# Closing the Tile frame behind the first transfer, and x in another shape and order, in a batched-expert kernel

## The chip, the core and the metric

The kernel runs on one core of a Trainium2 chip. Its time is the device time of one execution in microseconds (us). The span of a profile, from the first instruction to the last, is a little shorter than the time of the same execution. An engine here is one of TensorE (PE, its weight loads PEld), VectorE (DVE), ScalarE (ACT), GpSimd (POOL) and SyncE (SP). "q" behind a name (SPq, POOLq) marks the engine's instruction queue: semaphores, branches, drains, DMA issues.

## What is computed

```python
# x: 8 experts x 256 tokens x 512, w1: 8 x 512 x 2048, w2: 8 x 2048 x 512, all float32
h = np.matmul(x, w1)
h = np.maximum(h, 0)
return np.matmul(h, w2)          # 8 x 256 x 512, float32
```

## The kernel before

**Data.** The weights are float32 in HBM and arrive as bfloat16: POOL issues their DMAs, which convert on the way. `load_w1(e)` (L95) fetches 2 MB (counted as bfloat16) into one of two buffers, `load_w2(e)` (L98) the same; for the last expert w2 is fetched in two pieces (L103, L104). Each of 128 partitions gets one contiguous row of 16 KB per transfer, read from 32 KB in HBM. All of POOL's DMAs run through one queue (q0), in order; SP's run through another (q1). Both queues feed the same 16 DMA engines.

**x.** Experts 0 to 3 are fetched by SP as float32 (`x_f`, L82), experts 4 to 7 by POOL as bfloat16 (`x_c`, L106), each as one contiguous row of eight tokens per partition, 16 KB of HBM. ACT and DVE each bring one half into `x_b` (L156, L173; for the second group L160, L177). PE transposes `x_b` in four steps of eight 128x128 blocks (L203); DVE and ACT copy the four results out of PSUM in turns (`take_x`, L135; L147 and L145) into `xt`. Since eight tokens in a row lie in one partition, the tokens of one expert come out of the transposition scattered, and the copies write with a step of four elements (`"p m (q l) -> p l m q"`, L143). Both groups go through this before expert 0 begins; `give_xe` (L149) then copies one expert's columns into one of two buffers `xe`, which PE reads.

**Experts.** For each expert PE does 64 matmuls of the first layer (L215), in four quarters that go through two PSUM tensors; ACT and DVE apply the relu (L167, L185). Then come 32 matmuls of the second layer (L232), whose results DVE and ACT copy into `out_sb` (L189, L169).

**Order of the loads.** POOL issues x_c, w1(0), w2(0), builds the identity (L109 to L119), issues w1(1), w2(1), and then for each further expert waits until PE is done with the buffer: w1(e) is issued when the first layer of expert e-2 is done (L123), w2(e) when its second layer is done (L125). After the last weight it issues the outputs of experts 0 to 5 (L129) and of 6 (L132). SP stands in a row of waits (L83 to L89): each time a weight has landed it wakes and gives PE a token (`t_w`). Behind these waits it waits for the last result (L90, L91), issues the last expert's output (L92) and waits for all three outputs (L242).

**The frame.** The program stands inside a Tile frame (L269) and, in it, inside a critical section (L59) in which nothing is scheduled automatically. On entry SP signals the other engines (L59). On leaving, all engines report to SP (L59), then come, under L269, a drain of every engine, a barrier of all five, a clearing of the frame's semaphores by POOL, and a second barrier. The barrier at L258 is the program's own, ahead of the frame.

Of the kernel before, what the change touches and what calls it, by code (L numbers as in the profile page):

```python
# [9 lines left out]
def kernel(  # L10
# [48 lines left out]
    with tc.tile_critical(no_gpsimd_drain=True):  # L59
        sem = nc.alloc_semaphore  # L60
        s_x = [sem(f"s_x{g}") for g in range(2)]
        s_w1 = [sem(f"s_w1_{e}") for e in range(E)]
        s_w2 = [sem(f"s_w2_{e}") for e in range(E)]
        s_w2b = sem("s_w2b")
        s_out = [sem(f"s_out{i}") for i in range(3)]
        s_id = sem("s_id")
        s_act = sem("s_act")
        s_dve = sem("s_dve")
        s_tr = sem("s_tr")
        s_h = sem("s_h")  # L70
        s_o = sem("s_o")
        t_xb = sem("t_xb")
        t_pt = [sem(f"t_pt{b}") for b in range(2)]
        t_xe = sem("t_xe")
        t_w = sem("t_w")
        t_ha = sem("t_ha")
        t_hb = sem("t_hb")

        sp, pool, act, dve, pe = nc.sync, nc.gpsimd, nc.scalar, nc.vector, nc.tensor


        sp.dma_start(x_f[:], x_rows(0)).then_inc(s_x[0], 16)  # L82
        for e in range(E):  # L83
            sp.wait_ge(s_w1[e], 16).then_inc(t_w, 1)
            if e < E - 1:
                sp.wait_ge(s_w2[e], 16).then_inc(t_w, 2)
            else:
                sp.wait_ge(s_w2[e], 16).then_inc(t_w, 1)
                sp.wait_ge(s_w2b, 16).then_inc(t_w, 1)  # L89
        sp.wait_ge(s_act, E)  # L90
        sp.wait_ge(s_dve, E)  # L91
        sp.dma_start(out_r[:, E - 1], o_sb[:, E - 1]).then_inc(s_out[2], 16)  # L92


        def load_w1(e):  # L95
            pool.dma_start(w1_sb[e % 2][:], w1_r[e]).then_inc(s_w1[e], 16)  # L96

        def load_w2(e):  # L98
            if e < E - 1:
                pool.dma_start(w2_sb[e % 2][:], w2_r[e]).then_inc(s_w2[e], 16)  # L100
            else:
                b = w2_sb[e % 2]
                pool.dma_start(b[:, :CUT], w2_r[e, :, :CUT]).then_inc(s_w2[e], 16)  # L103
                pool.dma_start(b[:, CUT:], w2_r[e, :, CUT:]).then_inc(s_w2b, 16)  # L104

        pool.dma_start(x_c[:], x_rows(1)).then_inc(s_x[1], 16)  # L106
        load_w1(0)
        load_w2(0)
        pool.memset(identity[:], 0.0).then_inc(s_id, 1)  # L109
        pool.wait_ge(s_id, 1)  # L110
        pool.affine_select(
            out=identity[:],
            in_=identity[:],
            compare_op=mybir.AluOpType.not_equal,
            fill=1.0,
            base=0,
            pattern=[[-1, P]],
            channel_multiplier=1,
        ).then_inc(s_id, 1)  # L119
        load_w1(1)  # L120
        load_w2(1)
        for e in range(2, E):
            pool.wait_ge(s_h, NQ * (e - 1))  # L123
            load_w1(e)
            pool.wait_ge(s_o, MT * (e - 1))  # L125
            load_w2(e)
        pool.wait_ge(s_act, E - 2)
        pool.wait_ge(s_dve, E - 2)
        pool.dma_start(out_r[:, :E - 2], o_sb[:, :E - 2]).then_inc(s_out[0], 16)  # L129
# [5 lines left out]
        def take_x(g, half):  # L135

            for k in range(KT1):
                if k % 2 != half:
                    continue
                eng = act if half else dve  # L140
                eng.wait_ge(s_tr, g * KT1 + k + 1)
                src = pt[k % 2][:].rearrange("p (l m) q -> p l m q", m=MT)
                dst = xt[g][:, k].rearrange("p m (q l) -> p l m q", l=G)  # L143
                if half:
                    act.copy(dst, src).then_inc(t_pt[1], 1)  # L145
                else:
                    dve.tensor_copy(dst, src).then_inc(t_pt[0], 1)  # L147

        def give_xe(e):  # L149
            g, i0 = e // G, (e % G) * P  # L150
            dve.tensor_copy(xe[e % 2][:], xt[g][:, :, :, i0:i0 + P]).then_inc(t_xe, 1)  # L151


        HALF = J // 2
        act.wait_ge(s_x[0], 16)
        act.copy(x_b[:, :HALF], x_f[:, :HALF]).then_inc(t_xb, 1)  # L156
        take_x(0, 1)
        act.wait_ge(s_x[1], 16)
        act.wait_ge(s_tr, KT1)
        act.copy(x_b[:, :HALF], x_c[:, :HALF]).then_inc(t_xb, 1)  # L160
        take_x(1, 1)
        s_xt = sem("s_xt")
        act.drain().then_inc(s_xt, 1)  # L163
        for e in range(E):
            for q in range(0, NQ, 2):
                act.wait_ge(s_h, NQ * e + q + 1)
                act.activation(ht[e % 2][:, FB * q:FB * (q + 1), :], ph[0][:], relu).then_inc(t_ha, 1)  # L167
            act.wait_ge(s_o, MT * e + 2)
            act.copy(o_sb[:, e, 1, :], po[1][:]).then_inc(s_act, 1)  # L169


        dve.wait_ge(s_x[0], 16)
        dve.tensor_copy(x_b[:, HALF:], x_f[:, HALF:]).then_inc(t_xb, 1)  # L173
        take_x(0, 0)
        dve.wait_ge(s_x[1], 16)
        dve.wait_ge(s_tr, KT1)
        dve.tensor_copy(x_b[:, HALF:], x_c[:, HALF:]).then_inc(t_xb, 1)  # L177
        take_x(1, 0)
        dve.wait_ge(s_xt, 1)
        give_xe(0)  # L180
        give_xe(1)
        for e in range(E):
            for q in range(1, NQ, 2):
                dve.wait_ge(s_h, NQ * e + q + 1)
                dve.tensor_relu(ht[e % 2][:, FB * q:FB * (q + 1), :], ph[1][:]).then_inc(t_hb, 1)  # L185
            if e + 2 < E:
                give_xe(e + 2)
            dve.wait_ge(s_o, MT * e + 1)
            dve.tensor_copy(o_sb[:, e, 0, :], po[0][:]).then_inc(s_dve, 1)  # L189


        def take(s, n=1):
            pe.wait_ge(s, n).then_inc(s, -n)  # L193

        pe.wait_ge(s_id, 2)
        for b in range(2):
            pe.sem_inc(t_pt[b], 1)
        with pe.Fori(0, 2) as _g:
            take(t_xb, 2)
            for k in range(KT1):  # L200
                take(t_pt[k % 2])
                for j in range(J):
                    ins = pe.transpose(pt[k % 2][:, j], x_b[:, j, k::KT1], identity[:])  # L203
                ins.then_inc(s_tr, 1)

        with pe.Fori(0, E // 2) as _i:
            for b in range(2):
                take(t_xe)
                take(t_w)
                for q in range(NQ):  # L210
                    if q >= 2:
                        pe.wait_ge((t_ha, t_hb)[q % 2], 1)
                    for i in range(FB):
                        for kt in range(KT1):
                            ins = pe.matmul(  # L215
                                ph[q % 2][:, i, :],
                                w1_sb[b][:, kt, FB * q + i::KT2],
                                xe[b][:, kt],
                                start=(kt == 0),
                                stop=(kt == KT1 - 1),  # L220
                            )
                    ins.then_inc(s_h, 1)
                take(t_w)
                for kt in range(KT2):
                    if kt == 2 * FB:
                        take(t_ha, 2)
                    if kt == 3 * FB:
                        take(t_hb, 2)
                    if kt == CUT:
                        take(t_w)  # L230
                    for m in range(MT):
                        ins = pe.matmul(  # L232
                            po[m][:],
                            ht[b][:, kt, m * P:(m + 1) * P],
                            w2_sb[b][:, kt, :],
                            start=(kt == 0),
                            stop=(kt == KT2 - 1),
                        )
                        if kt == KT2 - 1:
                            ins.then_inc(s_o, 1)  # L240

        for s in s_out:  # L242
            sp.wait_ge(s, 16)


# [28 lines left out]
```

## Time and profile before

| | us |
|---|---|
| median of three runs | 184.15 |
| lowest and highest | 183.95, 184.28 |
| the profiled execution, its time | 184.07 |
| the profiled execution, its span | 182.3 |
| PE busy in it | 127.5 |
| DVE, ACT, POOL busy in it | 39.4, 35.7, 11.8 |

In the page of the profile the line that begins with DMA has one digit for each fortieth of the span: the mean busy share of the 16 DMA engines in tenths. GB/s counts the bytes as they are written, so that a float32 weight that lands as bfloat16 counts half of what was read. A "packet" is one row of a transfer on one DMA engine. In rows of a single line of the kernel, the three figures with strokes are the least, median and greatest duration in ns, and behind them stand the first and last start in us.

### The profile page before, as it was taken

Reading aid. Unit: us, or ns where it says so; the run is one execution under the profiler, and the core shown is the slowest. Engines: PE = TensorE matmul, PEld = TensorE weight load, DVE = VectorE, ACT = ScalarE, POOL = GpSimd, SP = SyncE. Lnnn points to the kernel's source line nnn. Section 1 sums busy time; section 2 is a strip of 40 time slices with the busy share of each in tenths; the row PEclk is TensorE's granted clock in tenths of the full one; section 3 lists DMA queues with packets and bytes.
Section 4 is the critical chain, followed back from the end, with each engine's and each line's share of the span. In section 5 each row is a group of like instructions: output and inputs, shape, how many; then the busy total and the mean of one; then the engine's idle time right before and its main releaser. Section 6 shows DMA issues by size and latency. Waiting matters only on the chain. (4 is left out here: it accounts for less than half of the span.)

```text
span 182.3 us, 1915 instructions
## 1 busy us (share of the span) xinstructions
PE 127.5 (70%) x832; PEld 90.0 (49%) x832; DVE 39.4 (22%) x38; ACT 35.7 (20%) x31; POOL 11.8 (6%) x26
## 2 busy tenths in 40 slices
PE   0006143999999794998677695949794989589910
PEld 0005142794794394339633682439642874198400
DVE  0025656023123123010501032012301040104010
ACT  2045856130230122002201220012201220122010
POOL 6100000001101101000101001010104000100000
PEclk9999999999999999699999999978999699999996
DMA  5999999999999999999999999999999999999990
GB/s 162 345 241 230 219 205 209 230 223 212 209 219 226 212 205 219 226 223 201 212 230 223 201 209 230 223 212 205 223 226 212 205 219 226 199 210 230 424 418 25
DMA packets 3810, 40.93 MB, mean 225 GB/s; under 512 B 352, under 2 KB 352, under 8 KB 1504
## 3 DMA queue, kind: packets, MB, share of 16 engines
q0 software_dynamic: 3520, 38.27, 94.2%
q1 hardware_dynamic: 288, 2.62, 4.0%
q8 instruction: 2, 0.03, 0.1%
HBM read 71.30 MB, written 4.19 MB: 414 GB/s over the span
## 5 line engine op out<-in xcount | busy, mean ns | idle before, releaser
L215 PE MATMUL pt_h<-xe,w_sb 128*128 128x256 bf16 x512 | 62.4, 286 | 15.8 <-PEq L193 15.8
L215 PEld LDWEIGHTS pt_h<-xe,w_sb 128*128 128x128 bf16 x512 | 58.6, 146 | 21.3 <-issue 18.9
L232 PE MATMUL pt_o<-w_sb,ht_sb 128*128 128x512 bf16 x256 | 58.2, 387 | 9.4 <-PEq L193 9.4
L232 PEld LDWEIGHTS pt_o<-w_sb,ht_sb 128*128 128x128 bf16 x256 | 25.2, 99 | 40.0 <-issue 12.6
L185 DVE TENSOR_SCALAR ht_sb<-pt_h 128x1024 bf16<-128x1024 f32 x16 | 19.6, 1224 | 61.7 <-PE pt_h L215 61.7
L167 ACT ACTIVATE ht_sb<-pt_h 128x1024 bf16<-128x1024 f32 x16 | 16.4, 1023 | 49.4 <-PE pt_h L215 49.4
L203 PE MATMUL pt_tr<-identity,x_b 128*128 128x128 bf16 x64 | 7.5, 308 | 21.4 <-PEq L193 21.4
L169 ACT COPY out_sb<-pt_o 128x512 f32<-128x512 f32 x8 | 4.7, 586 | 72.9 <-PE pt_o L232 72.9
L203 PEld LDWEIGHTS pt_tr<-identity,x_b 128*128 128x128 bf16 x64 | 6.4, 142 | 22.3 <-issue 22.1
L189 DVE COPY out_sb<-pt_o 128x512 f32<-128x512 f32 x8 | 5.5, 692 | 53.6 <-PE pt_o L232 53.6
L147 DVE COPY xt<-pt_tr 128x1024 bf16<-128x1024 bf16 x4 | 9.7, 2431 | 7.8 <-PE pt_tr L203 7.8
L145 ACT COPY xt<-pt_tr 128x1024 bf16<-128x1024 bf16 x4 | 9.7, 2434 | 6.8 <-PE pt_tr L203 6.8
L96 POOL DMA_DIRECT2D w_sb<-in_w_dram x8 | 4.3, 535 | 78.4 <-PE pt_h L215 78.2
L100 POOL DMA_DIRECT2D w_sb<-in_w_dram x7 | 3.7, 536 | 41.6 <-PE pt_o L232 41.6
L156 ACT CAST x_b<-x_f 128x2048 bf16<-128x2048 f32 x1 | 1.9, 1898 | 9.1 <-DMA x_f<-in_x_dram 9.1
L173 DVE CAST x_b<-x_f 128x2048 bf16<-128x2048 f32 x1 | 1.2, 1227 | 11.3 <-DMA x_f<-in_x_dram 11.3
L151 DVE COPY xe<-xt 128x1024 bf16<-128x1024 bf16 x8 | 3.3, 418 | 0.9 <-ACTq L163 0.9
L160 ACT COPY x_b<-x_c 128x2048 bf16<-128x2048 bf16 x1 | 2.0, 1957 | 0.0
L132 POOL DMA_DIRECT2D out_dram<-out_sb x1 | 0.5, 543 | 18.3 <-ACT out_sb L169 18.3
L156 ACT ACT_TABLE_LOAD x1 | 1.3, 1283 | 0.9 <-SPq L59 0.9
L103 POOL DMA_DIRECT2D w_sb<-in_w_dram x1 | 0.5, 528 | 7.5 <-PE pt_o L232 7.5
L129 POOL DMA_DIRECT2D out_dram<-out_sb x1 | 0.8, 846 | 0.0
(9 smaller groups left out, 2.8 us busy)
## 6 DMA issues: line engine op xcount, KB each, us to landing
w_sb<-in_w_dram POOLq DMA_DIRECT2D x15, 2048.0 KB, 30.3
out_dram<-out_sb POOLq DMA_DIRECT2D x1, 3072.0 KB, 37.7
x_f<-in_x_dram SPq DMA_DIRECT2D x1, 2048.0 KB, 10.3
w_sb<-in_w_dram POOLq DMA_DIRECT2D x1, 1152.0 KB, 27.0
x_c<-in_x_dram POOLq DMA_DIRECT2D x1, 1024.0 KB, 12.2
w_sb<-in_w_dram POOLq DMA_DIRECT2D x1, 896.0 KB, 30.8
out_dram<-out_sb POOLq DMA_DIRECT2D x1, 512.0 KB, 19.9
out_dram<-out_sb SPq DMA_DIRECT2D x1, 512.0 KB, 4.8
```

Source lines behind the costliest of these rows:

```text
L96: pool.dma_start(w1_sb[e % 2][:], w1_r[e]).then_inc(s_w1[e], 16)
L100: pool.dma_start(w2_sb[e % 2][:], w2_r[e]).then_inc(s_w2[e], 16)
L145: act.copy(dst, src).then_inc(t_pt[1], 1)
L147: dve.tensor_copy(dst, src).then_inc(t_pt[0], 1)
L151: dve.tensor_copy(xe[e % 2][:], xt[g][:, :, :, i0:i0 + P]).then_inc(t_xe, 1)
L167: act.activation(ht[e % 2][:, FB * q:FB * (q + 1), :], ph[0][:], relu).then_inc(t_ha, 1)
L169: act.copy(o_sb[:, e, 1, :], po[1][:]).then_inc(s_act, 1)
L185: dve.tensor_relu(ht[e % 2][:, FB * q:FB * (q + 1), :], ph[1][:]).then_inc(t_hb, 1)
L189: dve.tensor_copy(o_sb[:, e, 0, :], po[0][:]).then_inc(s_dve, 1)
L203: ins = pe.transpose(pt[k % 2][:, j], x_b[:, j, k::KT1], identity[:])
L215: ins = pe.matmul(ph[q % 2][:, i, :], w1_sb[b][:, kt, FB * q + i::KT2], xe[b][:, kt], start=(kt == 0), stop=(kt == KT1 - 1),)
L232: ins = pe.matmul(po[m][:], ht[b][:, kt, m * P:(m + 1) * P], w2_sb[b][:, kt, :], start=(kt == 0), stop=(kt == KT2 - 1),)
```

## The change

There are five edits, made together:

- The critical section holds only SP's first transfer. Behind it the frame is closed (`tc.close()`, `tc.compile()`), so that the frame's report, drains, barriers and clearing stand there, and everything else follows outside of any frame. The kernel ends with SP's waits for the outputs, and POOL's stream with a drain.
- x of experts 0 to 3 is fetched with two tokens of each of the four experts per partition: four rows of 4 KB in place of one of 16 KB. The tokens of an expert then come out of the transposition side by side, and the copies of the first group into `xt` write runs of 128 elements. The second group is as before.
- POOL's first three loads are w1(0), x_c, w2(0) in place of x_c, w1(0), w2(0).
- POOL writes the outputs of experts 0 to 3 after its last weight, and SP those of 4 to 6, in one transfer, and then, as before, that of 7.
- Three output semaphores and the two of x are allocated ahead of the frame's.

All loops, matmuls, relus and copies are otherwise the same and stand in the same order on their engines; the entries left out of the diff below are lines that only lose four blanks of indentation.

```diff
-    def x_rows(g):
-        return x[g * G:(g + 1) * G].rearrange("e c k -> (e c) k").rearrange(
-            "(p j) k -> p j k", p=P
-        )
+    x_rows = (
+        x[:G].rearrange("e (p m) k -> p e (m k)", p=P),
+        x[G:].rearrange("e c k -> (e c) k").rearrange("(p j) k -> p j k", p=P),
+    )
...
+    sem = nc.alloc_semaphore
+    s_x = [sem(f"s_x{g}") for g in range(2)]
+    s_out = [sem(f"s_out{i}") for i in range(3)]
     with tc.tile_critical(no_gpsimd_drain=True):
-        sem = nc.alloc_semaphore
...
-        sp.dma_start(x_f[:], x_rows(0)).then_inc(s_x[0], 16)
+        nc.sync.dma_start(x_f[:].rearrange("p (e m) k -> p e (m k)", m=MT), x_rows[0]).then_inc(s_x[0], 16)
+    tc.close()
+    tc.compile()
...
-        sp.wait_ge(s_act, E)
-        sp.wait_ge(s_dve, E)
-        sp.dma_start(out_r[:, E - 1], o_sb[:, E - 1]).then_inc(s_out[2], 16)
+    sp.wait_ge(s_act, E - 1)
+    sp.wait_ge(s_dve, E - 1)
+    sp.dma_start(out_r[:, G:E - 1], o_sb[:, G:E - 1]).then_inc(s_out[1], 16)
+    sp.wait_ge(s_act, E)
+    sp.wait_ge(s_dve, E)
+    sp.dma_start(out_r[:, E - 1], o_sb[:, E - 1]).then_inc(s_out[2], 16)
...
-        pool.dma_start(x_c[:], x_rows(1)).then_inc(s_x[1], 16)
-        load_w1(0)
-        load_w2(0)
+    load_w1(0)
+    pool.dma_start(x_c[:], x_rows[1]).then_inc(s_x[1], 16)
+    load_w2(0)
...
-        pool.wait_ge(s_act, E - 2)
-        pool.wait_ge(s_dve, E - 2)
-        pool.dma_start(out_r[:, :E - 2], o_sb[:, :E - 2]).then_inc(s_out[0], 16)
-        pool.wait_ge(s_act, E - 1)
-        pool.wait_ge(s_dve, E - 1)
-        pool.dma_start(out_r[:, E - 2], o_sb[:, E - 2]).then_inc(s_out[1], 16)
+    pool.wait_ge(s_act, G)
+    pool.wait_ge(s_dve, G)
+    pool.dma_start(out_r[:, :G], o_sb[:, :G]).then_inc(s_out[0], 16)
+    pool.drain()
...
-                dst = xt[g][:, k].rearrange("p m (q l) -> p l m q", l=G)
+            dst = xt[g][:, k].rearrange(
+                "p m (q l) -> p l m q" if g else "p m (l q) -> p l m q", l=G
+            )
...
-        for s in s_out:
-            sp.wait_ge(s, 16)
+    for s in s_out:
+        sp.wait_ge(s, 16)
```

More of the change, by code (lines that the diff above doesn't have):

```diff
@@ L66 @@
[L66 to L82, printed above, removed]
@@ L110 @@
[L110 to L126, printed above, removed]
@@ L149, in give_xe @@
[L149 to L189, printed above, removed]
@@ L192, in take @@
-        def take(s, n=1):
-            pe.wait_ge(s, n).then_inc(s, -n)
-        pe.wait_ge(s_id, 2)
-        for b in range(2):
[L197 to L231, printed above, removed]
@@ new lines @@
+        nc.sync.dma_start(x_f[:].rearrange("p (e m) k -> p e (m k)", m=MT), x_rows[0]).then_inc(s_x[0], 16)
+    tc.close()
+    tc.compile()
+    s_w1 = [sem(f"s_w1_{e}") for e in range(E)]
+    s_w2 = [sem(f"s_w2_{e}") for e in range(E)]
+    s_w2b = sem("s_w2b")
+    s_id = sem("s_id")
+    s_act = sem("s_act")
+    s_dve = sem("s_dve")
+    s_tr = sem("s_tr")
+    s_h = sem("s_h")
+    s_o = sem("s_o")
+    t_xb = sem("t_xb")
+    t_pt = [sem(f"t_pt{b}") for b in range(2)]
+    t_xe = sem("t_xe")
@@ new lines @@
+    t_w = sem("t_w")
+    t_ha = sem("t_ha")
+    t_hb = sem("t_hb")
+    sp, pool, act, dve, pe = nc.sync, nc.gpsimd, nc.scalar, nc.vector, nc.tensor
+    for e in range(E):
+        sp.wait_ge(s_w1[e], 16).then_inc(t_w, 1)
+        if e < E - 1:
+            sp.wait_ge(s_w2[e], 16).then_inc(t_w, 2)
+        else:
+            sp.wait_ge(s_w2[e], 16).then_inc(t_w, 1)
+            sp.wait_ge(s_w2b, 16).then_inc(t_w, 1)
+    sp.wait_ge(s_act, E - 1)
+    sp.wait_ge(s_dve, E - 1)
+    sp.dma_start(out_r[:, G:E - 1], o_sb[:, G:E - 1]).then_inc(s_out[1], 16)
@@ new lines @@
+    load_w1(0)
+    pool.dma_start(x_c[:], x_rows[1]).then_inc(s_x[1], 16)
+    load_w2(0)
+    pool.memset(identity[:], 0.0).then_inc(s_id, 1)
+    pool.wait_ge(s_id, 1)
+    pool.affine_select(
+        out=identity[:],
+        in_=identity[:],
+        compare_op=mybir.AluOpType.not_equal,
+        fill=1.0,
+        base=0,
+        pattern=[[-1, P]],
+        channel_multiplier=1,
+    ).then_inc(s_id, 1)
+    load_w1(1)
+    load_w2(1)
+    for e in range(2, E):
+        pool.wait_ge(s_h, NQ * (e - 1))
+        load_w1(e)
+        pool.wait_ge(s_o, MT * (e - 1))
+        load_w2(e)
@@ new lines, in give_xe @@
+    def give_xe(e):
+        g, i0 = e // G, (e % G) * P
+        dve.tensor_copy(xe[e % 2][:], xt[g][:, :, :, i0:i0 + P]).then_inc(t_xe, 1)
+    HALF = J // 2
+    act.wait_ge(s_x[0], 16)
+    act.copy(x_b[:, :HALF], x_f[:, :HALF]).then_inc(t_xb, 1)
+    take_x(0, 1)
+    act.wait_ge(s_x[1], 16)
+    act.wait_ge(s_tr, KT1)
+    act.copy(x_b[:, :HALF], x_c[:, :HALF]).then_inc(t_xb, 1)
+    take_x(1, 1)
+    s_xt = sem("s_xt")
+    act.drain().then_inc(s_xt, 1)
+    for e in range(E):
+        for q in range(0, NQ, 2):
+            act.wait_ge(s_h, NQ * e + q + 1)
+            act.activation(ht[e % 2][:, FB * q:FB * (q + 1), :], ph[0][:], relu).then_inc(t_ha, 1)
+        act.wait_ge(s_o, MT * e + 2)
+        act.copy(o_sb[:, e, 1, :], po[1][:]).then_inc(s_act, 1)
@@ new lines @@
+    dve.wait_ge(s_x[0], 16)
+    dve.tensor_copy(x_b[:, HALF:], x_f[:, HALF:]).then_inc(t_xb, 1)
+    take_x(0, 0)
+    dve.wait_ge(s_x[1], 16)
+    dve.wait_ge(s_tr, KT1)
+    dve.tensor_copy(x_b[:, HALF:], x_c[:, HALF:]).then_inc(t_xb, 1)
+    take_x(1, 0)
+    dve.wait_ge(s_xt, 1)
+    give_xe(0)
+    give_xe(1)
+    for e in range(E):
+        for q in range(1, NQ, 2):
+            dve.wait_ge(s_h, NQ * e + q + 1)
+            dve.tensor_relu(ht[e % 2][:, FB * q:FB * (q + 1), :], ph[1][:]).then_inc(t_hb, 1)
+        if e + 2 < E:
+            give_xe(e + 2)
+        dve.wait_ge(s_o, MT * e + 1)
+        dve.tensor_copy(o_sb[:, e, 0, :], po[0][:]).then_inc(s_dve, 1)
@@ new lines, in take @@
+    def take(s, n=1):
+        pe.wait_ge(s, n).then_inc(s, -n)
+    pe.wait_ge(s_id, 2)
+    for b in range(2):
+        pe.sem_inc(t_pt[b], 1)
+    with pe.Fori(0, 2) as _g:
+        take(t_xb, 2)
+        for k in range(KT1):
+            take(t_pt[k % 2])
+            for j in range(J):
+                ins = pe.transpose(pt[k % 2][:, j], x_b[:, j, k::KT1], identity[:])
+            ins.then_inc(s_tr, 1)
+    with pe.Fori(0, E // 2) as _i:
+        for b in range(2):
+            take(t_xe)
+            take(t_w)
+            for q in range(NQ):
+                if q >= 2:
+                    pe.wait_ge((t_ha, t_hb)[q % 2], 1)
+                for i in range(FB):
+                    for kt in range(KT1):
@@ L232 @@
                         ins = pe.matmul(
[L233 to L235 removed]
+                            ph[q % 2][:, i, :],
+                            w1_sb[b][:, kt, FB * q + i::KT2],
+                            xe[b][:, kt],
                             start=(kt == 0),
[L237 removed]
+                            stop=(kt == KT1 - 1),
                         )
[L239 to L240 removed]
@@ L242 @@
-        for s in s_out:
-            sp.wait_ge(s, 16)
+                ins.then_inc(s_h, 1)
+            take(t_w)
+            for kt in range(KT2):
+                if kt == 2 * FB:
+                    take(t_ha, 2)
+                if kt == 3 * FB:
+                    take(t_hb, 2)
+                if kt == CUT:
+                    take(t_w)
+                for m in range(MT):
+                    ins = pe.matmul(
+                        po[m][:],
+                        ht[b][:, kt, m * P:(m + 1) * P],
+                        w2_sb[b][:, kt, :],
+                        start=(kt == 0),
+                        stop=(kt == KT2 - 1),
+                    )
+                    if kt == KT2 - 1:
+                        ins.then_inc(s_o, 1)
```

51 lines of the change are left out of this document (19 added, 32 removed).

## The prediction

> **What bounds the kernel now.** I read the page first: busy shares, the DMA line, the HBM line.
>
> ```profile
> span 182.3 us, 1915 instructions
> ...
> PE 127.5 (70%) x832; PEld 90.0 (49%) x832; DVE 39.4 (22%) x38; ACT 35.7 (20%) x31; POOL 11.8 (6%) x26
> ...
> DMA  5999999999999999999999999999999999999990
> ...
> HBM read 71.30 MB, written 4.19 MB: 414 GB/s over the span
> ```
>
> No compute engine is full, and the DMA engines are from the second fortieth to the last but one. The DMA view of two stretches gives their pace, first with weights alone, then with outputs alone:
>
> ```profile
> DMA packets 2299, 32.43 MB, mean 216 GB/s; under 512 B 254, under 2 KB 254, under 8 KB 272
> ```
>
> ```profile
> DMA packets 836, 3.36 MB, mean 420 GB/s; under 512 B 16, under 2 KB 16, under 8 KB 836
> ```
>
> The first is 14 to 164 us. It counts bfloat16; from HBM twice as much was read, 432 GB/s. A row of 16 KB took 150 us x 16 engines / (2299 - 254) = 1.17 us of an engine. The second is 168.5 to 176.5 us, in rows of 4 KB: 420 GB/s, 8 x 16 / 820 = 0.156 us a row. So 4 KB rows run within 3% of the long ones. At these paces 71.3 MB take 165 us and 4.19 MB 10 us: 175 of the 182.3 us are bytes. The end is then set by when the DMA engines start, whether they ever run dry, and what follows the last byte. Next the end: SP's waits, the rows of the last instructions, and the DMA view of 178 to 180 us.
>
> ```profile
> 139.34 0.85 POOL L129 DMA_DIRECT2D out_dram<-out_sb  x1
> ...
> 174.73 0.35 SPq L92 DMA_DIRECT2D out_dram<-out_sb  x1
> ```
>
> ```profile
> SPq L243 <- DMA out_dram<-out_sb: 4.5, 1, 4.5
> ```
>
> ```profile
> L89 SPq EVENT_SEMAPHORE  x1: 17/17/17, 169.6 to 169.6; - x1
> ```
>
> ```profile
> L243 SPq EVENT_SEMAPHORE  x1: 28/28/28, 179.6 to 179.6; - x1
> ```
>
> ```profile
> L269 POOLq EVENT_SEMAPHORE  x4: 17/17/17, 181.7 to 182.2; - x4
> L269 POOLq DRAIN  x3: 45/78/1688, 179.9 to 182.0; - x3
> L269 SPq DRAIN  x3: 7/7/7, 180.2 to 181.9; - x3
> ```
>
> ```profile
> DMA packets 15, 0.04 MB, mean 20 GB/s; under 512 B 5, under 2 KB 5, under 8 KB 15
> ```
>
> SP wakes at 179.6, when the last output has landed. The rest, 2.7 us to 182.3, is the frame's end: POOL's drain from 179.9 (1.69 us) and two barriers, 181.7 and 182.2. The last row says that after 178 only 15 packets started: most engines are done and a straggler ends alone, about 1 us behind.
>
> **The change, part by part.**
>
> *The frame's end is taken from the end.* Minus 182.3 - 179.6 = 2.7 us. All that remains behind the last byte is SP's wait. POOL's new drain stands behind its last issue, which needs only w2(7)'s issue and results long there; in the trace POOL issues its outputs at 139. Were the drain 1.69 us, or as long as its DMAs run, SP's wait still ends later.
>
> *The frame's end is put at the start*, between SP's x issue and everything POOL does. The rows of the start:
>
> ```profile
> 0.95 0.38 SPq L82 DMA_DIRECT2D x_f<-in_x_dram  x1
> 1.46 0.67 POOL L106 DMA_DIRECT2D x_c<-in_x_dram  x1 [1.02 <-SPq L59]
> 2.13 0.55 POOL L96 DMA_DIRECT2D w_sb<-in_w_dram  x1
> ...
> 4.62 0.55 POOL L100 DMA_DIRECT2D w_sb<-in_w_dram  x1
> ...
> 11.26 1.90 ACT L156 CAST x_b<-x_f 128x2048 bf16<-128x2048 f32 x1 [9.06 <-DMA x_f<-in_x_dram]
> ```
>
> ```profile
> L269 POOLq COMPARE_BRANCH  x1: 33/33/33, 0.8 to 0.8; - x1
> ```
>
> ```profile
> L258 POOLq DRAIN  x1: 188/188/188, 0.3 to 0.3; - x1
> ```
>
> ```profile
> q1 hardware_dynamic: 78, 1.28, 68.4%
> ```
>
> ```profile
> q0 software_dynamic: 9, 0.07, 87.8%
> q1 hardware_dynamic: 2, 0.03, 19.2%
> ```
>
> SP's issue keeps its place and ends at 1.33. From SP's wake to its last drain ahead of the barrier were 180.2 - 179.6 = 0.6 us at the end: SP arrives at 1.9 to 2.0. From POOL's first event to its last, with clearing and second barrier, 0.5: POOL is free at 2.5. POOL's drain can start before SP comes, at about 0.9, with no DMA of its own yet. I take it as short, as the 188 ns of L258; were it 1.69 us, it would end at 2.6, and POOL be free at 3.1. Between its branch at 0.8 and its first DMA issue POOL spent 0.7 us, so w1(0) is issued at 2.5 to 3.8, with 0 to 0.7 of that; I take 2.9, against 1.46 for POOL's first DMA before. All engines but SP wait behind that barrier; ACT's table load (1.28 us) then ends by 4, long before x.
>
> What does that cost? The last two fences are the DMA view of 0 to 5.8 us and of 5.8 to 6.2. Until 5.8 only q1, which is x_f, moved; q0's first packet comes right after it, 4.4 us behind POOL's issue at 1.46. So x_f had the engines alone for nearly 4 us. 78 of its 128 rows had started, 1.28 of 2.1 MB; 16 were in flight, about half through. The remaining 0.82 + 0.13 MB at 432 GB/s are 2.2 us: alone, x_f would have ended at 8.0, and in 4 KB rows (3% slower) at 8.1. With w1(0) issued at 2.9 and the same 4.4 us, q0 moves from 7.3 (6.9 to 8.2 by the bounds). The DMA engines do not run dry in between, or by 0.1 us. All bytes are the same. **Cost: 0.15 us** for the 4 KB rows, 0 to 0.3 with the gap. The ramp (only 1.28 MB started by 5.8) may be better or worse with short rows: plus or minus 0.5, unknown, taken as 0.
>
> By the Trainium skill (DMA: Bandwidth & Descriptors, Latency and other measured facts) a DMA of POOL has its first byte after about 1 us and one of SP after about 0.6. This trace has 4.4 and about 1.0. By the page the overlap would be far larger; that case is the third rival.
>
> *x behind w1(0), and the copies.* These are before the first expert and touch the end only if the loads run dry. The chain of x and the cover, from the timeline and from L100:
>
> ```profile
> 14.50 2.43 DVE L147 COPY xt<-pt_tr 128x1024 bf16<-128x1024 bf16 x1 [2.02 <-PE pt_tr L203]
> ...
> 21.17 1.96 ACT L160 COPY x_b<-x_c 128x2048 bf16<-128x2048 bf16 x1
> ...
> 31.46 0.76 DVE L151 COPY xe<-xt 128x1024 bf16<-128x1024 bf16 x2 [0.92 <-ACTq L163]
> ```
>
> ```profile
> 41.39 0.53 POOL L96 DMA_DIRECT2D w_sb<-in_w_dram  x1 [36.22 <-PE pt_h L215]
> ```
>
> ```profile
> DMA to landing us min/median/max: 24.4/30.3/48.7
> ```
>
> ```profile
> q1 hardware_dynamic: 16, 0.00, 1.7%
> ```
>
> ```profile
> L167 ACT ACTIVATE ht_sb<-pt_h 128x1024 bf16<-128x1024 f32 x16 | 16.4, 1023 | 49.4 <-PE pt_h L215 49.4
> ```
>
> w1(2) is issued when expert 0's first layer is done, at 41.4; with 4.4 us it could move at 45.8. What is queued ahead ends with w2(1): issued at 4.62, landed 48.7 later, 53.3; a landing is seen about 1.3 us after the last byte (in 9.98 to 11.26 us, the fourth fence, q1 moved only 16 packets without bytes, so x_f's last row began before 10.0; it was seen at 11.26), so the engines have work until 52.0. The cover is 6.2 us. In the changed kernel the rest of x_f, w1(0) (4.19 MB) and x_c (2.1 MB) go from 7.3 on at 432 GB/s together: x_c ends at 8.1 + 9.7 + 4.9 = 22.7 and is seen at 24.0. Before, ACT took up the second group at 21.17 and xe came 10.3 us later; now it would be 34.3, later by 2.8 us. That uses 2.8 of the 6.2 us of cover, and without the cover it would be paid one for one. The copies of the first group should fall from 2.43 us to about 1.0 to 1.2 (an estimate from the row of 1024 contiguous results by ACT), 2.4 us of the first group's chain; it waits for x_c then. Value of both: 0.
>
> *The outputs.* SP issues experts 4 to 6 once w2(7)'s second piece has landed, since it stands behind that wait, and then expert 7. Bytes, rows and the moment at which the last result is ready (174.7) are the same. POOL's 2.1 MB follow w2 at once, in its queue, and keep the engines busy for 5 us; SP's 1.57 MB come beside them some 2 us after SP's wake at 169.6, well within that, and expert 7 arrives while they run. Value: 0, between -0.3 and +0.5, by how the straggler fares.
>
> **Sum:** 184.07 - 2.7 + 0.15 = 181.5 for the profiled execution, whose span would be 179.8. The median of the three runs is 0.08 above that execution: **181.6**.
>
> **The rivals.**
>
> *First: the start costs what the end saved.* If POOL's drain is 1.69 us and comes in series behind SP's arrival, or if the new branches stall, w1(0) is issued at 4.8 or later, moves at 9.2, and the engines idle from 8.1: +1.1, to 182.7; twice that, 183.8. Against it: POOL has nothing to drain and five engines went through the same barrier at L258 within 0.7 us.
>
> *Second: the change does not do what it says.* 184.07 - 182.3 = 1.77 us of the time lie outside the span. If what POOL drains, or what the frame cleared, is now done behind the last instruction, 1.7 to 2.5 of the 2.7 us come back there: 183.3 to 184.1. Against it: POOL has been drained and idle for 35 us by then. By the Trainium skill (Runtime: NRT & Kernel Launch, The ~15µs preamble/postamble breakdown) the runtime has a barrier and a reset of semaphores of its own behind the kernel. This trace shows nothing behind the span.
>
> *Third, and slower: x loses its turns.* Where both queues had work, 6 to 10 us, they took turns by packet:
>
> ```profile
> q0 software_dynamic: 56, 0.46, 54.6%
> q1 hardware_dynamic: 48, 0.79, 46.8%
> ```
>
> There both kinds of row took equally long, so it does not tell turns by row from turns by time. In the changed kernel a row of x_f is 0.156 us and one of w1(0) 1.17. By turns of rows, each row of x_f that is left per engine when w1(0) begins costs 1.33 us. At 7.3 five are left: x_f ends at 14, is seen at 15.3, and its group is done 21.2 - 11.3 - 2.4 = 7.5 us later, at 23, ahead of x_c. At 6.9, the lower bound, eight are left: seen at 18.4, xe at 18.4 + 20.2 - 2.4 = 36 (20.2 is 31.46 - 11.26): still under the cover. But if POOL's first data come as early as before, at 5.85, fourteen are left: eight turns against w1(0), six against x_c, to 5.85 + 8 x 1.33 + 6 x 0.75 = 21, seen at 22.3, xe at 40 (copies faster) to 42.5, w1(2) issued at 50 to 52.5, moving at 54.4 to 57 against 52: the engines idle for 2.5 to 5 us. At 181.6 that gives 184 to 186.6, in the middle 185.4. It becomes slower than before when xe is over 6.2 + 2.5 = 8.7 us late. For it: the 4.4 us may be a first start of POOL's that would not move with the barrier. By the Trainium skill (DMA: Bandwidth & Descriptors, Queues, rings and completion order) the engines do switch between queues at packets; no row here shows it for unequal ones.
>
> **How the numbers follow.** Forecast 0.70, 181.6, own range 180.9 to 182.3 (ramp and outputs). First rival 0.13, second 0.07, third 0.10. The range, 180.6 to 183.4, takes in the first rival's nearer part and, below, a straggler that catches up (-1.0); it leaves out the third, most of the second's upper half and the first's tail, under 0.2. A change of 0.2%, 0.37 us, is about what a measurement of this kernel can tell from none. Faster: 0.70 + 0.13 + 0.05 = 0.88; within: 0.02 of the second; slower: 0.10.
>
> **What would show it.** Right: SP's last wait ends near 179.8 and is the last row; q1 alone until about 7 us, then q0 without a gap; the first-group copies near 1.1 us; DMA line full from the second fortieth on. Wrong: a hole in the DMA line between x_f and w1(0) (first rival); a time far above span + 1.8 (second); x_f landing after 20 us and a hole near 52 (third).

## The result, and the profile after

| | before | changed |
|---|---|---|
| median of four runs, us | 184.12 | 181.08 |
| lowest and highest | 183.95, 184.28 | 180.45, 181.17 |
| the profiled execution: time, span | 184.07, 182.3 | 181.12, 179.8 |
| its time outside the span | 1.77 | 1.32 |

The ratio is 0.983 (95% interval 0.980 to 0.985): 3.0 us less. The forecast was 181.6, in a range of 180.6 to 183.4. One execution of the experiments below, 185.28 us with the frame closed before SP's first transfer, was over 1.5% slower than the fastest of the same kernel and is left out of its median and range.

The page of the changed kernel, the lines that answer to those of before:

```profile
span 179.8 us, 1898 instructions
...
PE 126.6 (70%) x824; PEld 89.4 (50%) x832; DVE 36.1 (20%) x38; ACT 32.9 (18%) x31; POOL 11.2 (6%) x25
...
DMA  5999999999999999999999999999999999999996
...
HBM read 71.30 MB, written 4.19 MB: 420 GB/s over the span
```

The bytes are those of before, and the DMA engines are full from the second fortieth on, now into the last one. Next, with their first and last start in us: SP's waits at the end (L254), POOL's drain behind its last output (L140), and rows of the frame's end, which now stands at the start (L69).

```profile
L254 SPq EVENT_SEMAPHORE  x2: 17/22/28, 178.5 to 179.8; - x2
```

```profile
L140 POOLq DRAIN  x1: 35915/35915/35915, 140.8 to 140.8; - x1
```

```profile
L69 POOLq EVENT_SEMAPHORE  x4: 17/17/17, 1.8 to 2.3; - x4
L69 POOLq DRAIN  x3: 34/41/65, 0.7 to 2.1; - x3
```

SP wakes at 179.8, and nothing follows in the span; before, SP woke at 179.6 and 2.7 us followed. At the start the two barriers and the clearing run from 1.8 to 2.3, and none of POOL's drains there is longer than 65 ns. POOL's drain at its new end lasts 35.9 us, to 176.7: it ends under SP's wait. The timeline of the start and of the chain of x:

```profile
0.95 0.43 SPq L67 DMA_DIRECT2D x_f<-in_x_dram  x1
...
2.90 0.67 POOL L106 DMA_DIRECT2D w_sb<-in_w_dram  x1 [2.45 <-POOLq L69]
...
18.58 1.23 DVE L184 CAST x_b<-x_f 128x2048 bf16<-128x2048 f32 x1 [18.58 <-DMA x_f<-in_x_dram]
...
21.83 0.69 DVE L158 COPY xt<-pt_tr 128x1024 bf16<-128x1024 bf16 x1 [2.02 <-PE pt_tr L214]
...
22.68 1.01 ACT L156 COPY xt<-pt_tr 128x1024 bf16<-128x1024 bf16 x1 [2.20 <-PE pt_tr L214]
...
35.87 0.76 DVE L162 COPY xe<-xt 128x1024 bf16<-128x1024 bf16 x2 [0.92 <-ACTq L174]
...
36.59 9.73 PE L226 MATMUL pt_h<-xe,w_sb 128*128 128x256 bf16 x64 [3.25 <-PEq L204]
...
46.62 0.53 POOL L106 DMA_DIRECT2D w_sb<-in_w_dram  x1 [40.02 <-PE pt_h L226]
```

POOL's first issue comes 1.4 us later than before. x of experts 0 to 3 is seen at 18.58 where it was 11.26, and w1(2) is issued at 46.6 where it was 41.4. None of that shows at the end. Counted by bytes, the transfers keep the pace of before: of 40.9 MB, 35.96 have begun by 164.2 us in the kernel before, and 36.00 by 164.4 in the changed one. The DMA view says why x is late: the first fence is 0 to 6.7 us, the second 8 to 17 (packets, MB, share of the 16 engines).

```profile
q1 hardware_dynamic: 386, 1.58, 67.5%
```

```profile
DMA packets 222, 2.23 MB, mean 248 GB/s; under 512 B 11, under 2 KB 11, under 8 KB 111
...
q0 software_dynamic: 111, 1.82, 94.5%
q1 hardware_dynamic: 111, 0.41, 12.1%
```

Until 6.7 only q1 moves, which is x_f. From 8 to 17 each queue has 111 packets: one of POOL's for one of SP's, though POOL's take 94.5% of the engines' time and SP's 12.1%. POOL's are all rows that land as 16 KB; of SP's 100 are rows of 4 KB and 11 are under 512 B. The engines take turns by packet, which is a row here, whatever its length.

### The profile page after: what moved, and what is told of

Its sections match the earlier page's. It is cut to its first block, busy times and chain, and to the rows that moved or that the text cites. A ratio compares the mean times of both kernels' runs of the same rounds, so it can differ in the third digit from the quotient of the medians.

```text
span 179.8 us, 1898 instructions
## 1 busy us (share of the span) xinstructions
PE 126.6 (70%) x824; PEld 89.4 (50%) x832; DVE 36.1 (20%) x38; ACT 32.9 (18%) x31; POOL 11.2 (6%) x25
## 5 line engine op out<-in xcount | busy, mean ns | idle before, releaser
L243 PE MATMUL pt_o<-w_sb,ht_sb 128*128 128x512 bf16 x248 | 59.5, 402 | 11.3 <-PEq L204 11.1
L226 PE MATMUL pt_h<-xe,w_sb 128*128 128x256 bf16 x512 | 59.9, 280 | 10.4 <-PEq L204 10.4
L226 PEld LDWEIGHTS pt_h<-xe,w_sb 128*128 128x128 bf16 x512 | 57.4, 146 | 14.4 <-issue 12.9
L243 PEld LDWEIGHTS pt_o<-w_sb,ht_sb 128*128 128x128 bf16 x256 | 25.9, 102 | 43.0 <-issue 17.4
L156 ACT COPY xt<-pt_tr 128x1024 bf16<-128x1024 bf16 x4 | 6.9, 1721 | 6.6 <-PE pt_tr L214 6.6
L158 DVE COPY xt<-pt_tr 128x1024 bf16<-128x1024 bf16 x4 | 6.2, 1561 | 7.7 <-PE pt_tr L214 7.7
L188 DVE COPY x_b<-x_c 128x2048 bf16<-128x2048 bf16 x1 | 0.7, 694 | 0.6 <-PE pt_tr L214 0.6
L139 POOL DMA_DIRECT2D out_dram<-out_sb x1 | 0.8, 766 | 0.0
```

Source lines behind the costliest of these rows:

```text
L226: ins = pe.matmul(ph[q % 2][:, i, :], w1_sb[b][:, kt, FB * q + i::KT2], xe[b][:, kt], start=(kt == 0), stop=(kt == KT1 - 1),)
L243: ins = pe.matmul(po[m][:], ht[b][:, kt, m * P:(m + 1) * P], w2_sb[b][:, kt, :], start=(kt == 0), stop=(kt == KT2 - 1),)
```

## The experiments

The theory: the end is set by when the DMA engines start, by whether they run dry, and by what follows the last byte. Closing the frame early takes its 2.7 us from the end and lays them under x_f; the new loads and outputs are worth nothing. The rivals: the loads or the outputs bring part of the gain, or the start still has to be paid. The edits below are against the changed kernel, except in the second and third, which are edits of the kernel before. Times are medians in us with the lowest and highest run, ratios are against the kernel before on the same chip, with their 95% interval.

### The frame alone

Only the frame's place and POOL's drain are new; rows, order and outputs are those of before. The edit also takes out SP's output of experts 4 to 6 and brings back the scattered copies.

```diff
-        x[:G].rearrange("e (p m) k -> p e (m k)", p=P),
+        x[:G].rearrange("e c k -> (e c) k").rearrange("(p j) k -> p j k", p=P),
...
-    load_w1(0)
     pool.dma_start(x_c[:], x_rows[1]).then_inc(s_x[1], 16)
+    load_w1(0)
...
-    pool.wait_ge(s_act, G)
-    pool.wait_ge(s_dve, G)
-    pool.dma_start(out_r[:, :G], o_sb[:, :G]).then_inc(s_out[0], 16)
+    pool.wait_ge(s_act, E - 2)
+    pool.wait_ge(s_dve, E - 2)
+    pool.dma_start(out_r[:, :E - 2], o_sb[:, :E - 2]).then_inc(s_out[0], 16)
+    pool.wait_ge(s_act, E - 1)
+    pool.wait_ge(s_dve, E - 1)
+    pool.dma_start(out_r[:, E - 2], o_sb[:, E - 2]).then_inc(s_out[1], 16)
```

> The changed kernel with the loads and the outputs of the kernel before: x in one 16 KB row per partition, x_c ahead of w1(0), POOL writing experts 0 to 5 and then 6. Only the place of the frame's end differs from the kernel before. Theory (the frame's end is the whole gain, the rest is worth nothing): 181.1, as the changed kernel, within 0.4. Rival A (the new order of the loads is what makes room for the frame at the start, since w1(0) in front hides the later start of POOL): 182 or more, with the DMA engines idle between x_f and x_c. Rival B (the outputs bring part of it): 181.5 to 182.

Measured: 180.92 (180.76 to 181.23), ratio 0.983 (0.981 to 0.986). The start and SP's last waits:

```profile
0.95 0.38 SPq L67 DMA_DIRECT2D x_f<-in_x_dram  x1
...
2.85 0.67 POOL L113 DMA_DIRECT2D x_c<-in_x_dram  x1 [2.40 <-POOLq L69]
...
10.73 1.23 DVE L182 CAST x_b<-x_f 128x2048 bf16<-128x2048 f32 x1 [10.73 <-DMA x_f<-in_x_dram]
...
30.93 0.76 DVE L160 COPY xe<-xt 128x1024 bf16<-128x1024 bf16 x2 [0.92 <-ACTq L172]
```

```profile
L252 SPq EVENT_SEMAPHORE  x2: 17/22/28, 178.5 to 179.8; - x2
```

The whole gain is there, with the old loads, and x is even a little earlier than before. Rivals A and B fall: the frame needs neither w1(0) in front nor the outputs.

### The new loads alone

The kernel before, with the 4 KB rows, their copies and w1(0) in front; the frame's end stays at the end.

```diff
-        sp.dma_start(x_f[:], x_rows(0)).then_inc(s_x[0], 16)
+        sp.dma_start(x_f[:].rearrange("p (e m) k -> p e (m k)", m=MT), x_rows[0]).then_inc(s_x[0], 16)
...
-        pool.dma_start(x_c[:], x_rows(1)).then_inc(s_x[1], 16)
         load_w1(0)
+        pool.dma_start(x_c[:], x_rows[1]).then_inc(s_x[1], 16)
```

> The kernel before with the new x alone: 4 KB rows of x for experts 0 to 3, their contiguous copies, and w1(0) ahead of x_c. The frame's end stays at the end, and POOL starts early. Theory: 184.1, within 0.4 of before, since the cover of w1(2) holds x; by turns of rows, x_f should be seen near 20 us, as POOL's first data come near 5.9 with about fourteen of its 32 rows per engine left, and x_f should bring xe at 38 or later; then w1(2) moves close to the time at which the engines run dry (52), so up to 1.5 us slower is possible (184.1 to 185.6). Rival (the loads bring part of the gain): 183.5 or less.

Measured: 185.43 (184.11 to 186.69), ratio 1.007 (1.004 to 1.010): slower. The profiled execution, 186.69, is the slowest of the ten. Its timeline:

```profile
21.75 1.23 DVE L175 CAST x_b<-x_f 128x2048 bf16<-128x2048 f32 x1 [21.75 <-DMA x_f<-in_x_dram]
...
39.20 0.76 DVE L153 COPY xe<-xt 128x1024 bf16<-128x1024 bf16 x2 [0.92 <-ACTq L165]
...
39.92 10.01 PE L217 MATMUL pt_h<-xe,w_sb 128*128 128x256 bf16 x64 [3.25 <-PEq L195]
...
50.23 0.53 POOL L96 DMA_DIRECT2D w_sb<-in_w_dram  x1 [45.06 <-PE pt_h L217]
```

One row of its stages by stretches of time, 52 to 53 us (the last three columns: granted clock, DMA share by packets begun, GB/s), and the same row of the changed kernel:

```profile
52.00:53.00 1.00, 1.00 (x6) 0.42 (x5) 0.00 (x0) 0.00 (x0) 0.00 (x0) 1.00 0.50 82
```

```profile
52.00:53.00 1.00, 1.00 (x6) 0.52 (x5) 0.00 (x0) 0.00 (x0) 0.00 (x0) 1.00 0.85 180
```

POOL begins early here, before x_f is through, so x_f loses more turns: seen at 21.75, xe at 39.2, w1(2) issued at 50.2. That is the third rival of the prediction, with its times (22.3, 40, 50), but without its hole of 2.5 to 5 us. A row of one us is too short to measure what is lost at 52, since the weights' rows take 1.2 us and begin together (the changed kernel has a share of 0.61 from 54 to 55). By bytes it is about 0.8 us: 35.96 MB have begun by 165.0 here, and by 164.2 in the kernel before. That is the smaller part of the profiled run's 2.6 us of longer span. The rest comes behind that, much of it at the end, where one engine of 16 (a share of 0.06) works alone for most of two microseconds, longer than the straggler of before:

```profile
180.00:181.00 1.00, 0.00 (x0) 0.00 (x0) 0.00 (x0) 0.00 (x0) 0.00 (x0) 0.50 0.06 25
181.00:182.00 1.00, 0.00 (x0) 0.00 (x0) 0.00 (x0) 0.00 (x0) 0.00 (x0) 0.50 0.05 20
```

### The new outputs alone

The kernel before, with POOL writing experts 0 to 3, and SP 4 to 6 and then 7.

```diff
+        sp.wait_ge(s_act, E - 1)
+        sp.wait_ge(s_dve, E - 1)
+        sp.dma_start(out_r[:, G:E - 1], o_sb[:, G:E - 1]).then_inc(s_out[1], 16)
         sp.wait_ge(s_act, E)
...
-        pool.wait_ge(s_act, E - 2)
-        pool.wait_ge(s_dve, E - 2)
-        pool.dma_start(out_r[:, :E - 2], o_sb[:, :E - 2]).then_inc(s_out[0], 16)
-        pool.wait_ge(s_act, E - 1)
-        pool.wait_ge(s_dve, E - 1)
-        pool.dma_start(out_r[:, E - 2], o_sb[:, E - 2]).then_inc(s_out[1], 16)
+        pool.wait_ge(s_act, G)
+        pool.wait_ge(s_dve, G)
+        pool.dma_start(out_r[:, :G], o_sb[:, :G]).then_inc(s_out[0], 16)
```

> The kernel before with the new outputs alone: POOL writes experts 0 to 3, SP writes 4 to 6 and then 7. Theory: 184.1, within 0.3 of before, since the same bytes keep the engines busy to the same moment. POOL's long drain at the frame's end should stay as it was, about 1.7 us, or become shorter if what it waits for is POOL's own last output, which now lands earlier. Rival (less of POOL's work at the end makes its drain short): 182.4 to 183.5.

Measured: 183.86 (183.25 to 184.02), ratio 0.9988 (0.9975 to 1.0001): at most 0.5 us, and not clear of none. The drain at its end:

```profile
L269 POOLq DRAIN  x3: 40/78/1615, 179.9 to 181.9; - x3
```

The drain stays, 1.62 us against 1.69, with less of POOL's work at the end. It is not POOL's last output that sets it; what does stays open.

### The long rows again

```diff
-        x[:G].rearrange("e (p m) k -> p e (m k)", p=P),
+        x[:G].rearrange("e c k -> (e c) k").rearrange("(p j) k -> p j k", p=P),
...
-                "p m (q l) -> p l m q" if g else "p m (l q) -> p l m q", l=G
+                "p m (q l) -> p l m q", l=G
```

> The changed kernel with x of experts 0 to 3 again in one 16 KB row per partition, and the scattered copies that belong to it. Theory of turns by row: x_f then has only one or two long rows per engine left when w1(0) begins at about 6.8, and is seen at 9.5 to 12 us instead of 18.6; xe comes near 34 to 35 (x_c sets it), and the time stays at 181.1, within 0.3, since all of it is under the cover. Rival (the queues share the engines by time or bytes, and x_f is late for another reason): x_f is again seen after 15. Rival (short rows or contiguous copies bring part of the gain): 181.6 or more.

Measured: 180.81 (180.47 to 181.86), ratio 0.985 (0.982 to 0.988).

```profile
12.25 1.23 DVE L182 CAST x_b<-x_f 128x2048 bf16<-128x2048 f32 x1 [12.25 <-DMA x_f<-in_x_dram]
...
33.46 0.76 DVE L160 COPY xe<-xt 128x1024 bf16<-128x1024 bf16 x2 [0.92 <-ACTq L172]
...
44.54 0.54 POOL L106 DMA_DIRECT2D w_sb<-in_w_dram  x1 [37.99 <-PE pt_h L224]
```

The same bytes in rows four times as long are seen 6.3 us earlier (18.58 to 12.25), with w1(0) in front in both. The theory had 9.5 to 12, and 12.25 is just behind it. Turns by row hold; sharing by bytes falls. The time is the same: the short rows and their copies bring nothing.

### x later still

```diff
     load_w1(0)
-    pool.dma_start(x_c[:], x_rows[1]).then_inc(s_x[1], 16)
     load_w2(0)
+    pool.dma_start(x_c[:], x_rows[1]).then_inc(s_x[1], 16)
```

> The changed kernel with x of experts 4 to 7 behind w2(0) as well, in the order w1(0), w2(0), x_c. x_c then ends 9.7 us later and is seen near 33.5, xe comes near 44 to 45, expert 0's first layer ends near 54, and w1(2) is issued there, when what is queued ahead runs dry near 52. Theory (the loads have about 1 us of cover left in the changed kernel, and beyond it each us is paid one for one): the DMA engines idle from 52 until w1(2) moves. If POOL's 3.9 to 4.4 us from issue to first data hold in mid-run, that is 58, and the time 187 (186 to 188). If the long start belongs to POOL's first DMA alone and a later one takes 1 to 1.5 us, the engines idle for about 3.5 us and the time is 184 to 185. Rival (the end does not hang on the loads): 181.1.

Measured: 185.79 (183.80 to 186.21), ratio 1.008 (1.005 to 1.012). The profiled run is the fastest of these, 183.80. Its timeline, and its DMA view of 51.9 to 54.0 in forty slices:

```profile
43.92 8.51 PE L226 MATMUL pt_h<-xe,w_sb 128*128 128x256 bf16 x64 [3.25 <-PEq L204]
...
52.72 0.53 POOL L106 DMA_DIRECT2D w_sb<-in_w_dram  x1 [46.13 <-PE pt_h L226]
```

```profile
DMA  0000000000000000000000000000000000000099
```

The engines are empty until the 39th slice: w1(2) is issued at 52.72 and moves at 53.9, 1.2 us later, not 4.4. POOL's long start belongs to its first DMA. The hole of about 2 us stands in the time: 183.80 is 2.7 above the changed kernel. By bytes the transfers lose more, 3.1 us (35.97 MB have begun by 167.5, against 36.00 by 164.4 in the changed kernel); 2.4 of it are left in the span, as here no engine ends behind the others. The rival (the end does not hang on the loads) falls. The median, 185.79, lies between the two forecasts and in neither, as the other runs are up to 2.4 us slower than the profiled one. Two more profiles of the same kernel were taken for that spread.

> The kernel with x later still, once more for its profile, to see where its slower executions lose up to 2.4 us. Theory: in a slower execution expert 0's first layer takes 9.5 to 10 us instead of 8.5, as the granted clock is lower there, w1(2) is issued that much later, and the hole grows by as much; the time follows it one for one. Rival: w1(2) comes at the same time and the loss is elsewhere, at the end for instance.

> The same kernel a third time, for the same reason: of the two executions at least one is likely to be a slower one. Theory and rival as for the other.

Measured, one execution each: 185.00 with a span of 183.5, and 185.52 with 184.2, where the first profile had 182.2. The rows of the first of them:

```profile
44.00 9.79 PE L226 MATMUL pt_h<-xe,w_sb 128*128 128x256 bf16 x64 [3.25 <-PEq L204]
...
54.09 0.53 POOL L106 DMA_DIRECT2D w_sb<-in_w_dram  x1 [47.50 <-PE pt_h L226]
```

There the theory holds: the first layer is 1.3 us longer, w1(2) is issued 1.4 later, and the span is 1.3 longer. But the granted clock is not the reason; the stretch with the slow matmuls has it at 1.00, as has the same stretch of the first profile, with 25 matmuls in place of 19:

```profile
44.00:48.00 4.00, 4.00 (x19) 3.20 (x20) 0.04 (x1) 0.35 (x1) 0.00 (x0) 1.00 1.07 229
```

In the second, w1(2) is issued at 53.06, only 0.3 later, and the rest is the rival's: SP's last wait ends at 184.2, and from 182 on one engine of 16 works alone:

```profile
182.00:183.00 1.00, 0.00 (x0) 0.00 (x0) 0.00 (x0) 0.00 (x0) 0.00 (x0) 1.00 0.06 25
```

So in these executions the spread has two sources, the pace of the first layer where the cover is gone, and how far the last DMA engine is behind. Why the pace differs and why one engine falls behind stays open.

### Without POOL's drain

```diff
     pool.dma_start(out_r[:, :G], o_sb[:, :G]).then_inc(s_out[0], 16)
-    pool.drain()
```

> The changed kernel without POOL's drain at its end. Theory (the drain ends under SP's wait): 181.1, within 0.3. Rival (the drain takes work off what follows the last instruction): up to 1.7 us more, 182.8, with the span unchanged at 179.8 and the difference behind it.

Measured: 180.97 (180.61 to 181.16), ratio 0.983 (0.980 to 0.986). The drain costs nothing and saves nothing, within the span or behind it.

### The frame closed before SP's first transfer

```diff
     with tc.tile_critical(no_gpsimd_drain=True):
-        nc.sync.dma_start(x_f[:].rearrange("p (e m) k -> p e (m k)", m=MT), x_rows[0]).then_inc(s_x[0], 16)
+        nc.sync.nop()
     tc.close()
     tc.compile()
...
+    sp.dma_start(x_f[:].rearrange("p (e m) k -> p e (m k)", m=MT), x_rows[0]).then_inc(s_x[0], 16)
```

> The changed kernel with the frame closed ahead of SP's first transfer too: the critical section holds only an empty instruction, and SP issues x_f behind the second barrier. Theory (the start of the DMA engines sets the end): x_f is issued later, at about 1.9 to 2.4 instead of 0.95, and everything behind it moves by as much: 182.0 to 182.6. POOL issues at about 2.4 to 2.9, as now or a little sooner. Rival (the start has slack, only the end counts): 181.1.

Measured: 182.73 (181.96 to 183.58), ratio 0.993 (0.991 to 0.996).

```profile
1.87 0.43 SPq L89 DMA_DIRECT2D x_f<-in_x_dram  x1
...
2.39 0.67 POOL L107 DMA_DIRECT2D w_sb<-in_w_dram  x1 [1.94 <-POOLq L69]
...
22.59 1.23 DVE L185 CAST x_b<-x_f 128x2048 bf16<-128x2048 f32 x1 [22.59 <-DMA x_f<-in_x_dram]
...
50.61 0.53 POOL L107 DMA_DIRECT2D w_sb<-in_w_dram  x1 [44.53 <-PE pt_h L227]
```

SP's issue is 0.92 us later and POOL's 0.5 earlier. The time is 1.65 above the changed kernel, a little more than forecast. x_f also loses more turns (seen at 22.59), so that w1(2) is issued at 50.6, as late as with the new loads alone; but in the profiled execution, 182.41, that costs nothing. Its transfers are 1.0 us behind those of the changed kernel by 35 us (7.98 MB have begun by 35.5, against 7.88 by 34.5), and still 1.0 at 165.4 (35.97 MB, against 36.00 at 164.4); the last 0.3 of its 1.3 us of longer span come behind that. So that x_f is issued ahead of the frame's end is worth about 1.0 us there. What the other executions lose beyond it was not measured.

### The frame and the outputs, with the old loads

The changed kernel with the rows of "the long rows again" and x_c ahead of w1(0).

```diff
-    load_w1(0)
     pool.dma_start(x_c[:], x_rows[1]).then_inc(s_x[1], 16)
+    load_w1(0)
```

> The changed kernel with the loads of the kernel before (16 KB rows of x, x_c ahead of w1(0)) and the new outputs: the frame's place and the outputs alone. Theory (the new loads give nothing and use up cover): not slower than the changed kernel, 180.6 to 181.1, with xe near 31 and w1(2) issued near 41.5, some 10 us ahead of the moment at which the engines would run dry. Rival (the new loads bring some of the gain): 181.5 or more.

Measured: 180.65 (180.58 to 181.56), ratio 0.983 (0.981 to 0.986).

```profile
30.68 0.76 DVE L160 COPY xe<-xt 128x1024 bf16<-128x1024 bf16 x2 [0.93 <-ACTq L172]
...
41.62 0.53 POOL L106 DMA_DIRECT2D w_sb<-in_w_dram  x1 [35.07 <-PE pt_h L224]
```

> The changed kernel unchanged, beside the others of this call on one chip: 181.1, within 0.3.

That run, on the same chip, gave 181.09 (180.92 to 181.29), ratio 0.984 (0.983 to 0.986). The version with the old loads has the lower median and 5 us more of cover, but the intervals overlap: that it is faster is not shown, only that the new loads are not needed.

### Rows of 2 KB

```diff
-        nc.sync.dma_start(x_f[:].rearrange("p (e m) k -> p e (m k)", m=MT), x_rows[0]).then_inc(s_x[0], 16)
+        for m in range(MT):
+            nc.sync.dma_start(x_f[:, m::MT], x[:G].rearrange("e (p m) k -> m p e k", p=P)[m]).then_inc(s_x[0], 16)
...
-    act.wait_ge(s_x[0], 16)
+    act.wait_ge(s_x[0], 16 * MT)
...
-    dve.wait_ge(s_x[0], 16)
+    dve.wait_ge(s_x[0], 16 * MT)
```

> The changed kernel with x of experts 0 to 3 in rows of 2 KB: two transfers, one for each of the two tokens of an expert in a partition. SP's second issue holds the frame's end up by some 0.4 us, so POOL issues at about 3.3 and w1(0) begins near 7.2. Theory of turns by row: about twelve rows per engine are left then; eight go against w1(0) (1.23 + 0.08 us a turn), the rest against x_c: x_f ends near 20, is seen at 21 to 22.5, later than the 18.6 of the 4 KB rows though its bytes are the same; xe near 39, w1(2) issued near 49 to 50, the time 181.1 to 182, the cover all but used. Rival (sharing by bytes or time): x_f is seen before 11, xe at 34.

Measured: 180.86 (180.63 to 182.16), ratio 0.985 (0.982 to 0.988).

```profile
3.46 0.67 POOL L107 DMA_DIRECT2D w_sb<-in_w_dram  x1 [3.01 <-POOLq L70]
...
17.09 1.23 DVE L185 CAST x_b<-x_f 128x2048 bf16<-128x2048 f32 x1 [17.09 <-DMA x_f<-in_x_dram]
```

x is seen at 17.1, not at 21 to 22.5. SP's second issue held POOL up, whose data began only after 7.6 us, by when x_f was nearly through; its DMA view of 0 to 7.6 us has 1.94 of 2.1 MB of x_f:

```profile
q1 hardware_dynamic: 961, 1.94, 70.8%
```

So few rows were left that the run does not tell the size of a turn. Sharing by bytes would still have had x seen before 11.

## Why the prediction was right

- **The frame's end, -2.7 us:** as forecast. SP's last wait is the last row, at 179.8, the span that the sum gave. The frame alone brings the whole gain, and POOL's drain is hidden, both shown by their own runs.
- **The start, +0.15 us:** POOL's issue at 2.9 was forecast and measured. POOL's first data came at 6.8 (after 6.7, only q1 before), inside 6.9 to 8.2 but for 0.1, since the start took 3.9 us in place of 4.4. The engines never ran dry, and SP's last wake came 0.2 us later than before.
- **Outside the span, taken as unchanged at 1.77:** this is the term that was mis-sized. It is 1.32 in the changed kernel, 1.43 with the frame alone, 1.27 with the long rows, against 1.79 and 1.81 with the frame's end at the end and new loads or new outputs. So 0.4 us more were saved, nearly all of the difference between 181.5 and 181.12 for the profiled execution. Over all executions on record it goes with the frame's place: its median is 1.34 in 49 with the frame closed early (four of them have 2.1 to 2.6) and 1.88 in 66 with the frame's end at the end. It is not POOL's drain, without which it is 1.36 as well; what it is was not tested.
- **The chain of x, value 0:** right in value, and late in its times. x_f was forecast at 15.3, or 18.4 at the bound of the earliest data, and seen at 18.58. xe was forecast at 34.3 to 36 and came at 35.9. The first-group copies fell from 2.43 to 0.69 on DVE and 1.01 on ACT, a little more than the estimate on DVE. w1(2) was issued at 46.6, later than the 44.2 that 2.8 us more would give: xe was 4.4 us later, and the first layer took 9.73 us in place of 8.9. The granted clock was lower in it (0.50, then 0.84), but that this is the reason is not shown: with the new loads alone the same 64 matmuls took 10.01 us at 1.00.

```profile
36.00:40.00 4.00, 3.41 (x17) 2.73 (x17) 0.63 (x2) 0.00 (x0) 0.00 (x0) 0.50 1.04 221
40.00:46.00 6.00, 6.00 (x48) 5.61 (x47) 1.22 (x1) 2.05 (x2) 0.00 (x0) 0.84 1.03 218
```

- **The cover, 6.2 us:** too small, because the 4.4 us of POOL's first DMA were put into mid-run. With the 1.2 us measured there, w1(2) could move at 42.6 before, and the cover was 9.4 by the prediction's count; the changed kernel has 52.0 - 46.6 - 1.2 = 4.2 left by it. That is somewhat too much: with the new loads alone w1(2) is issued 8.8 us later than before (50.2 against 41.4), and time is lost already. Two errors, a later x and a larger cover, stood on opposite sides; that the value came out at 0 is in part luck.
- **The outputs, value 0, between -0.3 and +0.5:** the outputs alone gave 0.26 less, not clear of none.
- **The rivals:** the first (a stall at the start) and the second (the cost comes back behind the span) did not occur. The argument against the second was wrong in one point: POOL was not drained and idle for 35 us, its drain ran to 176.7, 3.1 us ahead of SP's last wake. The third is real, not in this kernel but one edit away: with the loads alone it makes the kernel slower by 0.7% (0.4 to 1.0). What kept it out is the frame's end itself, which holds POOL up by 1.4 us while x_f moves alone. The rule quoted from the Trainium skill (DMA: Bandwidth & Descriptors, Queues, rings and completion order), turns by packet, holds here for unequal rows, with one row to a packet: 111 packets against 111. The first byte of POOL after about 1 us, by the Trainium skill (DMA: Bandwidth & Descriptors, Latency and other measured facts), agrees with the 1.2 in mid-run and not with the 3.9 to 4.4 at the start.

## What to carry to other kernels

Where transfers fill the run as they do here, look at three places first: the time before the first byte, any hole in the DMA line, and what follows the last byte. Fixed work that stands behind the last byte should be put under the first transfer, behind its issue and not ahead of it. Before short rows are set beside long ones in another queue, count their turns: each short row may wait for a long one, and that spends the cover which later loads need.

## What the runs showed of the hardware

- Two queues take turns packet by packet: 111 packets of SP's, 100 of them rows of 4 KB, and 111 rows of POOL's that land as 16 KB in the same 9 us, for 12.1% and 94.5% of the engines' time.
- POOL's first DMA of a run has its first data 3.8 to 4.4 us after its issue, one in mid-run, with the engines empty, 1.2 us after.
- POOL's drain takes 1.6 to 1.7 us when its transfers have landed, 35.9 us when they are under way, and 188 ns at most ahead of its first transfer.
- Without cover the runs spread: 184.1 to 186.7 with the new loads alone and 183.8 to 186.2 with x later still, against 180.8 to 181.2 with the frame alone and 180.5 to 181.9 with the long rows again. The same 64 matmuls of expert 0's first layer took 8.51 us in one execution of a kernel and 9.79 in another, at a granted clock of 1.00 from 44 to 48 us in both. Covered, such a delay costs nothing: the 9.73 us of the changed kernel do not show in the bytes moved, beyond 0.2 us.
- One or two of the 16 DMA engines end behind the others: one in the kernel before (the last row of 4 KB ends at 179.2), two in the changed kernel (a share of 0.12 from 178.4 to 179.2 us), and one with the new loads alone (0.06 from 180 to 181) and in the second repeat of x later still (0.06 from 182 to 183). With x later still, first profile, none did.
